# End of layer 1: a new order of tiles, T from scaled tiles, evictions in three operations, a last root without GpSimd

## The chip, the core and the metric

The kernel runs on one core of a Trainium2 chip. TensorE (PE) multiplies, VectorE (DVE), ScalarE (ACT) and GpSimd (POOL) do the elementwise work, SyncE (SP) mostly issues transfers. The metric is the device time of one execution in microseconds; the median of three is 2872.47 us.

## What is computed

A diffusion backbone of two layers over 1024 latent tokens of width 1024, with 256 context tokens. The change lies in the second layer, which has windowed attention and no context output; one helper of it, the output projection, is used by the first layer too. Of the reference, what follows the second layer's attention:

```python
def layer_norm(x, g, b):
    xf = x.astype(jnp.float32)
    mu = jnp.mean(xf, -1, keepdims=True)
    var = jnp.mean(jnp.square(xf - mu), -1, keepdims=True)
    return ((xf - mu) * lax.rsqrt(var + LN_EPS) * g + b).astype(x.dtype)

def modulate(x, shift, scale):
    return x * (1 + scale) + shift

def conv_ffn(h, w_up, conv_w, conv_b, w_down):
    u = h @ w_up
    L = u.shape[1]
    r = CONV_W // 2
    up = jnp.pad(u, ((0, 0), (r, r), (0, 0)))
    acc = conv_b
    for j in range(CONV_W):
        acc = acc + up[:, j:j + L] * conv_w[j]
    a, g = jnp.split(acc, 2, axis=-1)
    return (jax.nn.silu(g) * a) @ w_down
...
            y_lat, y_ctx = odd_mixer(h_lat, h_ctx, od_w_in[i], od_w_out[i], od_sink[i], cos, sin, ctx_out)
        x_lat = layer_norm(DN_ALPHA * x_lat + m_lat[2] * y_lat, ln_g[l, 0], ln_b[l, 0])
        f_lat = conv_ffn(modulate(x_lat, m_lat[3], m_lat[4]), ffn_w_up[l], ffn_conv_w[l], ffn_conv_b[l], ffn_w_down[l])
        x_lat = layer_norm(DN_ALPHA * x_lat + m_lat[5] * f_lat, ln_g[l, 1], ln_b[l, 1])
```

## The kernel before

Float32 values are multiplied as pairs: each operand is split into a high part (a cast to the matmul's type, on ACT) and a low part (value minus high part, a subtraction on DVE or POOL), and a product is three matmuls: high by high, high by low, low by high.

**Output projection** (`out_project`). The tokens are eight tiles of 128. For a tile t the mixer's output y is loaded in two halves into `yr` (L1425), cast to `yh` by ACT (L1426), and POOL subtracts into `yl` (L1427). 48 matmuls of 128x512 form two halves `o0` and `o1`. DVE evicts a half in three operations: times the gate (L1446), plus alpha times x (L1447), statistics (L1450). `ln` then forms the mean and the reciprocal root, which it calls rs (DVE L360, POOL L362 and L363), and normalises x (DVE L376; for the last tile half on ACT, L375). `finish` of the tile before, which calls `build_B1`, stands behind a tile's matmuls; for the last tile it stands in the middle of them. A scheduler orders this section's instructions on each engine from the program's order.

**Operand of the up product** (`build_B1`). The normalised tile is transposed by TensorE (L1728, tile `tr`) and modulated by ACT (L1734). Tiles 0 to 3 are the left and 4 to 7 the right half of the token axis; features are split too, so the operand has four blocks: `h3la` and `h3lb` (with `h` and `l` behind the name for the high and low part). For the seven products of a Strassen-like scheme, four differences T0 to T3 of the blocks are needed. They are formed when tile t of 4 to 7 is there, from its own modulated values and from the high and low parts of tile t - 4, six DVE operations (L1768 to L1773), and stored to DRAM; tile 7's stay on chip in `w` buffers. Later they are loaded again (`gk`, `go`, `ua`, `ug`), and split into T0h, T0l and so on (L1871, L1872).

After the last tile TensorE runs `first_x` (two products over tiles 0 to 3, which starts with L2928), the last tile's transposes, and `rest` (two further products).

**Up stage** (`ffn7`, from here on in an order written out by hand). 22 pairs of feature blocks; a pair is seven products of twelve matmuls (L1842) into tiles x, y, q, v. ACT and DVE form u from them (among others L2479, which q waits for), convolve (`centre` on ACT, `sides` on DVE, L2321), apply Silu (ACT, L2349), multiply (L2353), and `store` and `mix` form the sums that the down product reads, which `put` sends to DRAM through POOL's queue. Two pairs share a buffer, `gk` of the even and `go` of the odd one; slots 0 to 6 of the store are the seven products' left operands.

**Down stage.** 77 pieces (11 by seven products), each of twelve matmuls on four tiles (L2524). `load(j)` brings two pieces' right and left operands and splits them (right: L112 and L113, left: L2301 and L2302). The order of everything else is a table of jobs by the piece's number: `job(i, f)` issues f behind piece i. `evict` moves a result to z, in three operations (L2534, L2538, L2539), or with a saved part `vs` in four (L2536 to L2539). `end` is the final layer norm (L360, then POOL L362 and L363, then DVE L3088 and L3091, then the store L3093). The last nine pieces run tile by tile, 4 to 7, each followed by its eviction and `end`:

```python
            for t in range(4):
                for i in range(NS - last, NS):
                    mm(i, t)
                evict(4 + t, 0, Y[t])
                end(4 + t)
```

## Time and profile before

| | us |
|---|---|
| median of three runs | 2872.47 (2872.45 to 2876.41) |
| the profiled execution | 2874.48, its span 2872.6 |
| PE busy | 2747.7 (96% of the span) |
| DVE busy | 2145.0 (75%) |
| ACT busy | 1388.0 (48%) |
| POOL busy | 667.2 (23%) |

Times in rows count from the span's start. The section at hand runs from about 2110 to the end: projection to 2206, up stage to about 2640, down stage behind it. In the rows, `x12` is a count, and a bracket `[2.87 <-issue]` is how long the engine was idle before and what ended that. The ends of matmuls are modelled, so the spacing of starts (0.227 us for 128x512) is the surer measure.

### The profile page before, as it was taken

What the parts mean: (1) busy time and instruction counts of PE and PEld (TensorE: products, weight loads), DVE (VectorE), ACT (ScalarE), POOL (GpSimd) and SP (SyncE); (2) the same over time, 40 slices, a digit from 0 to 9 for tenths busy, and PEclk for the clock granted to TensorE, in tenths of its full rate; (3) what the DMA queues carried; (4) which work ended last, traced back from release to release, by engine and by line L of the source; (5) the groups of instructions that cost most, each with busy time, mean ns of one, the idle gap of its engine ahead of it and who ended that gap; (6) DMA issues with size and microseconds to landing.
All of it is one profiled execution on the core that took longest, in us unless ns stands there. A gap on an engine that the chain in (4) does not pass through costs nothing.

```text
span 2872.6 us, 45400 instructions
## 1 busy us (share of the span) xinstructions
PE 2747.7 (96%) x16724; PEld 2244.9 (78%) x16724; DVE 2145.0 (75%) x3852; ACT 1388.0 (48%) x2607; POOL 667.2 (23%) x948
## 2 busy tenths in 40 slices
PE   8999799899999999999999999999998999999997
PEld 6787577777789988888888888766677788888886
DVE  4765676667588777888878656677778888888778
ACT  4321255567435655455553344167743555445541
POOL 4501243354451000000001002255644011111002
PEclk9999899999999999999999999999999999999998
DMA  7568611032558753333458525652244355555962
GB/s 272 153 206 279 214 32 43 9 134 92 169 161 243 216 165 108 110 114 110 121 197 294 173 98 171 199 165 81 83 132 162 120 180 176 165 173 205 329 218 90
DMA packets 369222, 457.02 MB, mean 159 GB/s; under 512 B 26008, under 2 KB 265016, under 8 KB 367464
## 3 DMA queue, kind: packets, MB, share of 16 engines
q1 hardware_dynamic: 341512, 369.53, 40.5%
q0 software_dynamic: 24592, 82.89, 8.3%
q8 instruction: 131, 2.15, 0.3%
q10 hardware_dynamic: 2896, 1.70, 0.2%
q14 instruction: 91, 0.75, 0.1%
HBM read 338.11 MB, written 115.93 MB: 158 GB/s over the span
## 4 chain that ended last, share of the span: by engine, by line
PE 70%; DVE 9%; issue 9%; DMA 5%; ACT 4%; POOL 2%; SPq 0%; ACTq 0%; POOLq 0%; DVEq 0%
PE q L1842 8%; PE x L1842 7%; PE y L1842 7%; PE S L882 4%; PE v L1842 4%; PE pv L1027 3%; PE mm L405 3%; PE mm L407 3%; PE mm L406 3%; PE T L1013 3%; PE dy L2524 3%; PE d L407 3%; PE d L406 3%; PE d L405 3%; PE dx L2524 2%
## 5 line engine op out<-in xcount | busy, mean ns | idle before, releaser
L906 POOL TENSOR_SCALAR P<-P,rin 128x640 f32<-128x640 f32 (+3 forms) x288 | 253.0, 882 | 333.8 <-DVE rin L905 301.8
L1816 DVE TENSOR_TENSOR w<-raw,w 128x512 fp32r<-128x512 f32 x308 | 208.6, 691 | 90.1 <-ACT w L1814 89.9
L113 DVE TENSOR_TENSOR w<-raw,w 128x512 fp32r<-128x512 f32 x315 | 204.5, 689 | 86.4 <-ACT w L112 83.1
L112 ACT CAST w<-raw 128x512 fp32r<-128x512 f32 x315 | 183.4, 620 | 173.4 <-PE d L407 67.2
L882 PE MATMUL S<-k,q 64*128 64x256 f32 (+2 forms) x1824 | 194.9, 337 | 17.3 <-DVE nm L2862 8.3
L903 ACT ACTIVATE P<-P,nm 128x641 f32<-128x641 f32 (+4 forms) x208 | 161.5, 778 | 84.9 <-DVE nm L2862 43.9
L1814 ACT CAST w<-raw 128x512 fp32r<-128x512 f32 x308 | 182.3, 620 | 15.1 <-DVE raw L1821 9.9
L882 PEld LDWEIGHTS S<-k,q 64*128 64x128 f32 x1824 | 136.9, 187 | 54.5 <-issue 19.1
L893 ACT COPY PT<-T 128x512 f32<-128x512 f32 (+1 forms) x250 | 134.9, 566 | 82.7 <-PE T L1013 80.0
L1027 PE MATMUL pv<-PT,v 128*64 128x128 f32 x2016 | 132.9, 279 | 16.6 <-ACT PT L893 13.9
L1013 PE MATMUL T<-ident,P 128*128 128x128 f32 x1008 | 135.8, 282 | 9.5 <-POOL P L906 3.3
L1027 PEld LDWEIGHTS pv<-PT,v 128*64 128x64 f32 x2016 | 108.5, 137 | 42.7 <-ACT PT L893 23.2
L405 PE MATMUL d<-w,w 128*128 128x512 f32 x352 | 137.5, 391 | 0.0
L407 PE MATMUL d<-w,w 128*128 128x512 f32 x352 | 137.0, 389 | 0.0
L406 PE MATMUL d<-w,w 128*128 128x512 f32 x352 | 137.0, 389 | 0.0
L1013 PEld LDWEIGHTS T<-ident,P 128*128 128x128 f32 x1008 | 110.4, 142 | 29.8 <-issue 17.4
L891 DVE COPY PT<-T 128x512 f32<-128x512 f32 (+1 forms) x166 | 110.4, 666 | 31.0 <-PE T L1013 21.1
L905 DVE RECIPROCAL rin<-den 128x1 f32<-128x1 f32 x288 | 46.0, 161 | 112.1 <-ACT P L903 108.7
L1842 PE MATMUL q<-T3h,w 128*128 128x512 f32 x352 | 121.1, 405 | 7.6 <-DVE ug L2479 4.0
L2524 PE MATMUL dy<-w,w 128*128 128x512 f32 x528 | 120.7, 390 | 0.0
L1842 PE MATMUL q<-T2h,w 128*128 128x512 f32 x352 | 115.9, 390 | 2.3 <-ACT q L2461 1.8
L903 ACT ACTIVATE P<-P,mc 128x1280 f32<-128x1280 f32 (+1 forms) x80 | 94.7, 1186 | 46.0 <-DVE mc L1148 41.6
(450 smaller groups left out, 7779.6 us busy)
## 6 DMA issues: line engine op xcount, KB each, us to landing
raw<-in_up_dram SPq DMA_DIRECT2D x132, 512.0 KB
raw<-in_down_dram SPq DMA_DIRECT2D x59, 512.0 KB
raw<-g SPq DMA_DIRECT2D x44, 512.0 KB
raw<-G SPq DMA_DIRECT2D x38, 512.0 KB
araw<-in_ada_w_dram SPq DMA_DIRECT2D x32, 512.0 KB
raw<-in_w_in_dram SPq DMA_DIRECT2D x28, 512.0 KB
g<-cv POOLq DMA_DIRECT2D x22, 512.0 KB, 3.0
G<-go POOLq DMA_DIRECT2D x44, 256.0 KB, 2.7
```

Of the source, the lines that this page charges most:

```text
L113: (lo_eng or nc.vector).tensor_sub(lo, s, f32(hi))
L405: nc.tensor.matmul(ps, lh, rh, start=first, stop=False)
L406: nc.tensor.matmul(ps, lh, rl, start=False, stop=False)
L407: nc.tensor.matmul(ps, ll, rh, start=False, stop=last)
L882: self.nc.tensor.matmul(outs[a], q[r, x, qs], k[r, y, ks], start=(i == 0), stop=(i == 2))
L903: nc.scalar.activation(P[:, :m], P[:, :m], AF.Exp, bias=negm, scale=-1.0, accum_out=den)
L906: nc.gpsimd.tensor_scalar(P[:, :n], P[:, :n], rin, 1.0, ALU.mult, ALU.mult)
L1013: nc.tensor.transpose(ps[:, s * 128 : (s + 1) * 128], P[a][:, cols[i + x] : cols[i + x] + 128], self.ident,)
L1027: nc.tensor.matmul(O[a * HD : (a + 1) * HD], v_of(a, vts[i + x]), pT[:, s * 128 : (s + 1) * 128], start=(i + x == 0), stop=(i + x == m - 1 ...
L1816: nc.vector.tensor_sub(half(i, 1), src[i], f32(half(i, 0)))
L1842: nc.tensor.matmul(ps, w[:, a, s], r[b][:, k], start=first and k + i == 0, stop=k == 3 and i == 2, skip_group_check=True,)
L2524: nc.tensor.matmul(banks[q][t], ga[i][:, a, c], wd[i][:, b], start=q < 2 and f + k == 0, stop=f == HF - 1 and k == 2, skip_group_check=True,)
```

## The change

1. `out_project` drops `yr`: y is loaded into `yl` and the subtraction is done in place. The tiles of layer 1 run in the order 0, 4, 1, 5, 2, 6, 3, 7. The first layer's projection keeps its order and gets the load in place.
2. `build_B1`: the low part's subtraction (L1746) goes from POOL to DVE. The modulated values of a tile below 4 stay in a buffer `b` until tile t + 4 follows, and T is formed from these in four DVE operations. Only tile 7 keeps T on chip; tile 6 stores it as the others do.
3. `rest` begins with a Silu of one column, so the table of Silu is loaded there.
4. In an odd pair the sum for slot 0 and its store go from `store` to the start of `mix`, which in the instruction order is behind L2479.
5. Down stage: every seventh load's right operands lie in a pool of their own with two buffers, the left operands have seven buffers, loads run up to six ahead where they ran up to five, and reach the next depth sooner; the scaling of z (`scale`) and of the norm's rows (`alpha`) are early; `gated` multiplies the saved part by the gate and `shared` adds it to z before the evictions, which then take three operations each. The norm's rows of the last layer norm are loaded into the tiles of the first.
6. The table of Sqrt is loaded behind the last copies of ACT. The last tile has an `end` of its own: Sqrt on ACT, reciprocal on DVE, five operations on one column on ACT (one step that refines the root), and the last multiply and store in two halves on two queues. GpSimd takes no part in it.

The order of DVE at three places. First, tiles 6 and 7 in the projection: `hst<-o1` is the eviction of tile 7's right half; `hst` and `b` are modulated values. Before:

```order
L1768 TENSOR_TENSOR yh_23551<-hst_23534,h3lah_22713 128x512
L1769 TENSOR_TENSOR yh_23551<-yh_23551,h3lal_22714 128x512
L1745 CAST h3lbh_22715<-hst_23544 128x4x128
L1770 TENSOR_TENSOR yh_23551<-hst_23544,yh_23551 128x512
L1771 TENSOR_TENSOR yl_23552<-hst_23544,hst_23534 128x512
L1772 TENSOR_TENSOR yl_23552<-h3lbh_22715,yh_23551 128x512
L1773 TENSOR_TENSOR yl_23552<-yl_23552,h3lbl_22716 128x512
L1446 TENSOR_TENSOR hst_23586<-o_4548_23487,gate_22733 128x512
L1447 SCALAR_TENSOR_TENSOR x_23488<-x_23488,hst_23586 128x512
```

Now, with tile 3 ahead of tile 7:

```order
L1745 CAST h3lah_22695<-b_23502 128x4x128
L1746 TENSOR_TENSOR h3lal_22696<-b_23502,h3lah_22695 128x4x128
L1745 CAST h3lbh_22697<-b_23514 128x4x128
L1746 TENSOR_TENSOR h3lbl_22698<-b_23514,h3lbh_22697 128x4x128
L1446 TENSOR_TENSOR hst_23546<-o_4519_23457,gate_22715 128x512
L1447 SCALAR_TENSOR_TENSOR x_23458<-x_23458,hst_23546 128x512
```

Six T operations and a cast stood ahead of the eviction; two casts and two subtractions stand there now. Second, DVE from tile 7's T to T0l. Before:

```order
L1768 TENSOR_TENSOR w_23653<-hst_23636,h3lah_22713 128x512
L1769 TENSOR_TENSOR w_23653<-w_23653,h3lal_22714 128x512
L1745 CAST h3lbh_22715<-hst_23646 128x4x128
L1770 TENSOR_TENSOR w_23653<-hst_23646,w_23653 128x512
L1771 TENSOR_TENSOR w_23654<-hst_23646,hst_23636 128x512
L1772 TENSOR_TENSOR w_23654<-h3lbh_22715,w_23653 128x512
L1816 TENSOR_TENSOR w_23687<-raw_22956,w_23687 128x512
L1773 TENSOR_TENSOR w_23654<-w_23654,h3lbl_22716 128x512
L1816 TENSOR_TENSOR w_23690<-raw_22956,w_23690 128x512
L1872 TENSOR_TENSOR T0l_23717<-gk_23718,T0h_23716 128x2x4x128
```

Now (L1802 is L1816 of before, L1858 is L1872):

```order
L1761 TENSOR_TENSOR w_23613<-hst_23596,b_23502 128x512
L1745 CAST h3lbh_22697<-hst_23606 128x4x128
L1762 TENSOR_TENSOR w_23613<-hst_23606,w_23613 128x512
L1746 TENSOR_TENSOR h3lbl_22698<-hst_23606,h3lbh_22697 128x4x128
L1763 TENSOR_TENSOR w_23614<-hst_23606,hst_23596 128x512
L1764 TENSOR_TENSOR w_23614<-b_23514,w_23613 128x512
L1802 TENSOR_TENSOR w_23647<-raw_22934,w_23647 128x512
L1802 TENSOR_TENSOR w_23650<-raw_22934,w_23650 128x512
L1858 TENSOR_TENSOR T0l_23677<-gk_23678,T0h_23676 128x2x4x128
```

Ahead of T0l stand eight operations where nine stood, one of them the low part that POOL formed. Third, the last tile's eviction and norm on DVE. Before:

```order
L2534 TENSOR_TENSOR tt_28658<-dy_5059_27073,gate_27054 128x512
L2538 TENSOR_TENSOR z_5033_27041<-z_5033_27041,tt_28658 128x512
L2539 BN_STATS s_5041_27049<-z_5033_27041 128x6
L360 BN_AGGR mv_28662<-s_5041_27049 128x2
L3088 SCALAR_TENSOR_TENSOR z_5033_27041<-z_5033_27041,mv_28662,lg_27845 128x1024
L3091 SCALAR_TENSOR_TENSOR z_5033_27041<-z_5033_27041,rs_28664,lb_27846 128x1024
```

Now:

```order
L2527 TENSOR_TENSOR tt_28630<-dy_5028_27036,gate_27017 128x512
L2528 TENSOR_TENSOR z_5002_27004<-z_5002_27004,tt_28630 128x512
L2529 BN_STATS s_5010_27012<-z_5002_27004 128x6
L3088 BN_AGGR mv_28634<-s_5010_27012 128x2
L3091 TENSOR_SCALAR lv_28636<-mv_28634 128x1
L3092 RECIPROCAL ly_28637<-ly_28637 128x1
L3093 SCALAR_TENSOR_TENSOR z_5002_27004<-z_5002_27004,mv_28634,gb_5019_27027 128x1024
L3103 SCALAR_TENSOR_TENSOR z_5002_27004<-z_5002_27004,lr_28640,gb_5020_27028 128x512 x2
```

The reciprocal waits for ACT ahead of the wide operation, and the last multiply is two halves.

The diff, its context cut:

```diff
@@ -98,12 +98,12 @@
-    def split(self, src, n, shape=None, lo_eng=None):
+    def split(self, src, n, shape=None, lo_eng=None, pool=None):
...
         for s in src:
-            w = self.t(self.ring, [128, 2, 512], "w", R)
+            w = self.t(pool or self.ring, [128, 2, 512], "w", R)
             hi, lo = w[:, 0, :n], w[:, 1, :n]
@@ -1420,8 +1420,8 @@
                 for q in range(2):
-                    yr = self.t(st, [128, 4, 128], "yr", bufs=2)
                     s = slice(4 * q, 4 * q + 4)
+                    yr = f32(yl[:, s])
                     nc.sync.dma_start(yr, yv[:, s, t * 128 : (t + 1) * 128])
@@ -1728,7 +1728,7 @@
                 )
-            s = self.t(st, [128, 4, 128], "hst", bufs=3)
+            s = self.t(st, [128, 4, 128], "b" if t < 4 else "hst", bufs=2 if t < 4 else 3)
             for j in range(4):
@@ -1743,8 +1743,9 @@
             nc.vector.tensor_copy(h, s)
-            nc.gpsimd.tensor_sub(l, s, f32(h))
+            nc.vector.tensor_sub(l, s, f32(h))
         if t < 4:
+            self.b1 = sg
             return
@@ -1752,31 +1753,16 @@
             self.tlast = tt = [m[i // 2][:, i % 2] for i in range(4)]
-        elif t == NLAT - 2:
-            m = [
-                self.t(st, [128, KT, 128], x, bufs=2).rearrange("p (m k) j -> p m k j", m=2)
-                for x in ("yh", "yl")
-            ]
-            tt = [m[i // 2][:, i % 2] for i in range(4)]
         else:
...
             tt = [m[:, i] for i in range(4)]
-        b11, b21 = ([f32(v) for v in x] for x in (
-            (ah[:, :, o], al[:, :, o]), (bh[:, :, 0, o], bl[:, :, 0, o])
-        ))
+        b11, b21 = self.b1
         b12, b22 = sg
-        nc.vector.tensor_sub(tt[0], b12, b11[0])
-        nc.vector.tensor_sub(tt[0], tt[0], b11[1])
+        nc.vector.tensor_sub(tt[0], b12, b11)
         nc.vector.tensor_sub(tt[1], b22, tt[0])
         nc.vector.tensor_sub(tt[2], b22, b12)
-        nc.vector.tensor_sub(tt[3], b21[0], tt[1])
-        nc.vector.tensor_add(tt[3], tt[3], b21[1])
-        if t == NLAT - 2:
-            for i in range(2):
-                nc.gpsimd.dma_start(
-                    dT[2 * i : 2 * i + 2, :, t - 4].rearrange("m p k j -> p m k j"), m[i]
-                )
-        elif t < NLAT - 2:
+        nc.vector.tensor_sub(tt[3], b21, tt[1])
+        if t < NLAT - 1:
             nc.gpsimd.dma_start(dT[:, :, t - 4].rearrange("m p k j -> p m k j"), m)
@@ -2240,7 +2226,7 @@
     def ffn7(self, l, B, hps, T, dT, xsrc, gate_row, view, begin, finish, norm,
-             early=None, px=None):
+             early=None, px=None, warm=None):
@@ -2291,7 +2277,8 @@
                 nc.sync.dma_start(g[:, :m], Gv[:, s : s + m])
-                for i, w in enumerate(self.split([r[:, i] for i in range(m)], 512)):
+                pool = wp if j >= 3 and j % 7 == 6 else self.ring
+                for i, w in enumerate(self.split([r[:, i] for i in range(m)], 512, pool=pool)):
                     wd[s + i] = w
@@ -2357,13 +2344,13 @@
                     put(6, f, x[:, 512:])
-                    k = half["k"]
-                    nc.vector.tensor_add(k[:, 512:], k[:, 512:], x[:, 512:])
-                    put(0, f, k[:, 512:])
...
                     f, x, k = s.i // 2, s.a, half["k"]
-                    if s.i % 2 == 0:
+                    if s.i % 2:
+                        nc.vector.tensor_add(k[:, 512:], k[:, 512:], x[:, 512:])
+                        put(0, f, k[:, 512:])
+                    else:
                         nc.vector.tensor_sub(k[:, :512], k[:, :512], k[:, 512:])
@@ -2501,7 +2488,8 @@
             zp = es.enter_context(self.pool("fz"))
-            gp[0] = es.enter_context(self.pool("fgs", bufs=6))
+            gp[0] = es.enter_context(self.pool("fgs", bufs=7))
+            wp = es.enter_context(self.pool("fws", bufs=2))
             pd = es.enter_context(self.pool("fd", space=PSUM))
@@ -2527,14 +2515,16 @@
-            def evict(t, n, ps, v=None):
+            def gated(t):
+                nc.vector.tensor_mul(vs[t], vs[t], gate[:, 512:])
+
+            def shared(t):
+                nc.vector.tensor_add(z[t][:, 512:], z[t][:, 512:], vs[t % 4])
+
+            def evict(t, n, ps):
                 s = slice(n * 512, (n + 1) * 512)
                 tt = self.t(tt2, [128, 512], "tt")
-                if v is None:
-                    nc.vector.tensor_mul(tt, ps, gate[:, s])
-                else:
-                    nc.vector.tensor_add(tt, v, ps)
-                    nc.vector.tensor_mul(tt, tt, gate[:, s])
+                nc.vector.tensor_mul(tt, ps, gate[:, s])
                 nc.vector.tensor_add(z[t][:, s], z[t][:, s], tt)
@@ -2566,22 +2556,25 @@
                 job(8 + 3 * t, lambda t: nc.sync.dma_start(z[t], xsrc(t)), t)
-                job((20 + 3 * t) if t < 4 else (46 + 2 * (t - 4)), scale, t)
-            job(16, alpha)
-            job(36, begin, es, pd)
+                job(14 + 3 * t, scale, t)
+                job(37 + 2 * t, shared, t)
+            job(12, alpha)
+            job(36, begin, es, pd, gb)
             job(HF - 1, copies, vs, Y)
...
                 job(3 * HF + 1 + 2 * t, evict, t, 0, X[t])
-                job(5 * HF + 2 * t, evict, t, 1, Y[t], vs[t])
+                job(33 + t, gated, t)
+                job(5 * HF + 2 * t, evict, t, 1, Y[t])
                 job(5 * HF + 1 + 2 * t, end, t)
-                job(6 * HF + t // 2, evict, 4 + t, 1, X[t], vs[t])
+                job(6 * HF + t // 2, evict, 4 + t, 1, X[t])
+            job(6 * HF + 1, warm)
             ahead = 2
...
                 if i % 2 == 0:
-                    n = i // 2 + min(5, 2 + i // 12)
+                    n = i // 2 + min(6, 2 + i // 10)
                     while ahead <= n:
@@ -2930,12 +2923,14 @@
             def rest():
+                warm = self.t(st, [128, 1], "warm")
+                nc.scalar.activation(warm, self.mhalf[:, :1], AF.Silu)
                 for p in range(2):
...
             self.out_project(
-                io["w_out1"], d["yT1"], list(range(8)),
+                io["w_out1"], d["yT1"], [0, 4, 1, 5, 2, 6, 3, 7],
                 rows("x2"), lambda t: gate, finish, st, wx, pp,
@@ -3073,15 +3068,47 @@
-        def begin_o(es, pd):
+        def begin_o(es, pd, gb):
             st = box["st"] = es.enter_context(self.pool("fino"))
-            box["g"] = self.t(st, [128, D], "lg")
-            box["b"] = self.t(st, [128, D], "lb")
+            box["g"], box["b"] = gb
             self.bcast(box["g"], io["ln_g"][1, 1])
             self.bcast(box["b"], io["ln_b"][1, 1])
+            box["c"] = self.t(st, [128, 4], "lc")
+            for i, v in enumerate((LN_EPS, -1.25, 1.875, 1.0)):
+                nc.vector.memset(box["c"][:, i : i + 1], v)
+
+        def warm_o():
+            nc.scalar.activation(
+                self.t(box["st"], [128, 1], "warm"), box["c"][:, 3:], AF.Sqrt
+            )
+
+        def last_o(t, z, s6):
+            st, c = box["st"], box["c"]
+            mv = self.t(st, [128, 2], "mv", bufs=3)
+            nc.vector.bn_aggr(mv, s6.rearrange("p a b -> p (a b)"))
+            ve, y, e, p, rs = (self.t(st, [128, 1], "l" + x) for x in ("v", "y", "e", "p", "r"))
+            nc.scalar.activation(y, mv[:, 1:2], AF.Sqrt, bias=c[:, :1])
+            nc.vector.tensor_scalar(ve, mv[:, 1:2], LN_EPS, 1.0, ALU.add, ALU.mult)
+            nc.vector.reciprocal(y, y)
+            nc.vector.scalar_tensor_tensor(
+                z, z, mv[:, 0:1], box["g"], ALU.subtract, ALU.mult
+            )
+            nc.scalar.activation(e, y, AF.Identity, scale=y)
+            nc.scalar.activation(e, e, AF.Identity, scale=ve)
+            nc.scalar.activation(p, e, AF.Identity, bias=c[:, 1:2], scale=0.375)
+            nc.scalar.activation(p, p, AF.Identity, bias=c[:, 2:3], scale=e)
+            nc.scalar.activation(rs, p, AF.Identity, scale=y)
+            for h, q in enumerate((nc.sync, nc.scalar)):
+                s = slice(h * 512, (h + 1) * 512)
+                nc.vector.scalar_tensor_tensor(
+                    z[:, s], z[:, s], rs, box["b"][:, s], ALU.mult, ALU.add
+                )
+                q.dma_start(io["out"][t * 128 : (t + 1) * 128, s], z[:, s])
...
             st = box["st"]
+            if t == NLAT - 1:
+                return (lambda: last_o(t, z, s6)), None
             mv, rs = self.stats(st, s6)
@@ -3095,7 +3122,7 @@
         self.ffn7(1, h2l, [hl, pxc], {}, d["T1"], rows("x3"), a[1, 0, 5], view1, begin_o, finish_o,
-                  (io["ln_g"][1, 0], io["ln_b"][1, 0]), early=self.early, px=px)
+                  (io["ln_g"][1, 0], io["ln_b"][1, 0]), early=self.early, px=px, warm=warm_o)
         self.finish_dbg()
...
     def finish_dbg(self):
```

## Prediction

> **What bounds the kernel now.** I read the windows by stage first, then the waits of TensorE in the stretch that the change touches, then the time rows around each wait, and last the chain at the end. The windows give busy time per engine; the columns are PE, PEld, DVE, ACT, POOL, granted clock, DMA share, GB/s.
>
> ```profile
> 2110.00:2260.00 150.00, 134.81 (x598) 108.89 (x597) 115.56 (x154) 60.19 (x126) 53.56 (x56) 0.97 0.44 146
> 2260.00:2640.00 380.00, 379.75 (x1665) 311.24 (x1663) 332.38 (x436) 195.36 (x298) 60.30 (x112) 1.00 0.54 171
> 2640.00:2793.00 153.00, 152.18 (x669) 125.37 (x669) 115.73 (x139) 79.05 (x114) 3.77 (x7) 1.00 0.80 283
> 2793.00:2854.00 61.00, 60.93 (x269) 50.13 (x267) 55.13 (x74) 14.33 (x21) 13.30 (x16) 1.00 0.29 104
> ```
>
> From 2260 to 2854 TensorE is never idle (379.75 of 380, 152.18 of 153, 60.93 of 61). So a microsecond that leaves the front (2110 to 2260, where 15.2 us of PE are missing and the clock is 0.97) reaches the end unless a feeder runs out, and behind 2854 nothing is left but the last tiles' tail. What TensorE waits for in the front:
>
> ```profile
> PE v L1842 <- DVE T0l L1872: 4.6, 1, 4.6
> PE q L1842 <- DVE ug L2479: 3.0, 1, 3.0
> PE tr L1728 <- issue: 2.9, 1, 2.9
> ...
> PE tr L1728 <- DVE x L376: 0.7, 1, 0.7
> ```
>
> These four are 11.2 of the 15.2 us, and DVE stands behind each.
>
> **Part A, the transposes (L1728).** The waits of 0.7 and 2.9 stand ahead of the transposes of a normalised tile: the first of tile 6, in the middle of tile 7's matmuls, the second of tile 7. Below are DVE's and TensorE's rows around the second.
>
> ```profile
> 2199.97 0.67 DVE L1768 TENSOR_TENSOR yh<-hst,h3lah 128x512 f32<-128x512 f32 x1
> ...
> 2205.26 0.68 DVE L1446 TENSOR_TENSOR hst<-o,gate 128x512 f32<-128x512 f32 x1
> ```
>
> ```profile
> 2200.45 0.39 PE L2928 MATMUL y<-h3lah 128*128 128x512 f32 x1
> ...
> 2209.38 1.06 PE L1728 MATMUL tr<-ident,x 128*128 128x128 f32 x8 [2.87 <-issue]
> ```
>
> TensorE left tile 7 at 2200.45 (L2928 is the first matmul of what follows, the product on tiles 0 to 3), but the eviction of tile 7's right half (L1446) stood on DVE behind tile 6's whole T, from 2199.97 to 2205.26. In the new order tile 3 is ahead of tile 7, has no T, and hands DVE two casts and two subtractions; the eviction then starts near 2201, 4 us sooner, against a wait of 2.9. Both waits go: 3.6 us. Bounds: 0 if the four short operations of tile 3 come as late as tile 6's did, 3.6 at most. That product on tiles 0 to 3 now reads tile 3, made just before; if its low part were late, that would wait in place of this, but DVE reaches it ahead of the eviction. I take 3.6.
>
> **Part B, T0l (L1872).** T0l is the low half of the first of the four T, read by tile 0 to 3's v product; a quarter of it comes from tile 7. DVE's rows, and TensorE's wait:
>
> ```profile
> 2211.64 0.69 DVE L1768 TENSOR_TENSOR w<-hst,h3lah 128x512 f32<-128x512 f32 x1 [2.37 <-ACT hst L1734]
> ...
> 2213.99 1.80 DVE L1771 TENSOR_TENSOR w<-hst,hst 128x512 f32<-128x512 f32 x1
> ```
>
> ```profile
> 2221.19 0.50 PE L1842 MATMUL v<-T0l,w 128*128 128x512 f32 x1 [4.55 <-DVE T0l L1872]
> ```
>
> From tile 7's first T operation to TensorE's start DVE runs without a gap, 2211.64 to 2221.19. Two subtractions like L1768 go (0.69 each, 1.3 together by start to start). L1771 takes 1.80 while GpSimd subtracts the low part; with that subtraction on DVE it should take the 0.68 of its neighbours, 1.1 less, and the subtraction itself adds 0.7. Net 1.7, which I take; bounds 0.6 (if L1771 stays at 1.80) and the whole 4.55.
>
> **Part C, the Silu table and the clock.** ACT's rows in the second pair of the up stage:
>
> ```profile
> 2248.03 1.28 ACT L2349 ACT_TABLE_LOAD   x1 [2.41 <-DVE cv L2321]
> 2249.32 1.06 ACT L2349 ACTIVATE cv<-cv 128x1024 f32<-128x1024 f32 x1
> ```
>
> The load stands between DVE's convolution and Silu, and DVE's product, the q ahead of TensorE (L2479) and the wait of 3.0 stand behind it. Issued early it falls into a stretch of ACT that waits for y anyway, so 1.28 goes and the wait becomes 1.7. [...] I stay with 1.28.
>
> The second cost of the wait is the clock. Two windows with a granted clock of 0.50, then pieces of the chain:
>
> ```profile
> 2221.79:2225.20 3.41, 3.41 (x10) 2.65 (x9) 3.41 (x5) 0.00 (x0) 0.00 (x0) 0.50 0.90 312
> 2252.50:2259.30 6.80, 5.90 (x14) 4.64 (x15) 3.85 (x7) 0.38 (x1) 1.12 (x2) 0.50 0.20 77
> ```
>
> ```profile
> 2253.40 5.49 PE q L1842 x12
> 2258.88 3.01 PE x L1842 x12
> ...
> 2275.49 2.95 PE q L1842 x12
> ```
>
> Behind the waits of 4.55 and 3.0 TensorE ran at 0.50 for 3.41 and 6.80 us; behind 2.87 it did not. The 5.90 us of work in the second stretch cost 2.95 too much (5.49 + 3.01 against 5.44 gives 3.06). A wait of 1.7 is below the 2.87 that left the clock alone, so I take 2.9 here; bounds 0 and 3.06. B's wait stays near 2.9, where either may happen: I count nothing, with 1.7 (half of 3.41) as the upper bound. [...]
>
> **Part D, odd pairs of the up stage.** DVE's rows in one odd pair, and the last of the slow q pieces of the chain beside a normal one:
>
> ```profile
> 2312.40 0.69 DVE L2361 TENSOR_TENSOR gk<-gk,go 128x512 f32<-128x512 f32 x1
> 2313.01 0.68 DVE L2479 TENSOR_TENSOR ug<-ua,q 128x512 f32<-128x512 f32 x1
> ```
>
> ```profile
> 2579.78 2.72 PE y L1842 x12
> 2582.50 2.98 PE q L1842 x12
> ```
>
> The sum for slot 0 (L2361) stands ahead of the operation on which q waits, and in eight odd pairs, from 2275.49 (2.95) to 2582.50 (2.98), q's twelve matmuls show some 0.22 above 2.72. The sum moves behind L2479, 0.6 by start to start, which covers 0.22: 8 x 0.22 = 1.8. It adds work before the next pair's convolution writes the same buffer, whose store must have landed first:
>
> ```profile
> G<-go POOLq DMA_DIRECT2D x44, 256.0 KB, 2.7
> ```
>
> In the new order some six DVE operations of 0.6 lie between the two, about 3.6 us by estimate, so 2.7 fits, narrowly; a landing at 4.6 would cost each even pair 1, which ACT's idle share there (195 busy of 380) would partly take. I take 1.6; bounds -1 and 1.8.
>
> **Part E, the tail.** TensorE's last group, two split pieces of the chain, and DVE's rows of evictions and of the last root:
>
> ```profile
> 2828.84 25.09 PE L2524 MATMUL dy<-w,w 128*128 128x512 f32 x110
> ```
>
> ```profile
> 2828.74 1.28 DVE w L113 x2
> 2830.02 1.14 DVE w L2302
> ```
>
> ```profile
> 2843.35 0.68 DVE L2534 TENSOR_TENSOR tt<-dy,gate 128x512 f32<-128x512 f32 x1
> ...
> 2860.23 0.68 DVE L2534 TENSOR_TENSOR tt<-dy,gate 128x512 f32<-128x512 f32 x1
> ...
> 2864.64 1.28 DVE L3091 SCALAR_TENSOR_TENSOR z<-z,rs,lb 128x1024 f32<-128x1024 f32 x1 [0.72 <-POOL rs L363]
> ```
>
> TensorE ends at 2853.9, and the last eviction starts only at 2860.2: 6.3 us of DVE backlog. Tile 4's (2843.35) is late by 8.2, its matmuls being done near 2835.1 (25.09 us for 110 matmuls is 0.228 each, and a tile's last nine pieces are 27 of them, 6.2 us; three tiles behind tile 4 make 18.5 to 18.8 before 2853.9). The change takes one of four operations out of eight right-half evictions (8 x 0.70 = 5.6) and, with loads one deeper, moves one load's splits (1.28 + 1.14 = 2.4) ahead of 2793. That is 8.0 of the 8.2. What is moved ahead, twelve operations of 0.7 and the splits, 11 us, lies in the window 2640:2793, where DVE is busy 115.73 of 153 and its cover is 37 us. From tile 4 on DVE needs 5.6 a tile ((2860.23 - 2843.35)/3) and TensorE 6.2, so the rest of the backlog melts, and the last eviction starts when TensorE ends: 6.2 us (bounds 0 and 6.3).
>
> Behind it the end changes too:
>
> ```profile
> L3204 POOLq DRAIN  x3: 46/93/7784, 2864.0 to 2872.3; - x3
> ```
>
> ```profile
> 2865.95 0.33 SPq L3093 DMA_DIRECT2D out_dram<-z  x1
> ```
>
> ```profile
> L2758 ACT ACTIVATE warm<-snk 128x1 f32<-128x1 f32 x1 | 0.2, 203 | 0.5 <-DVE snk L2618 0.5
> ```
>
> GpSimd's closing drain starts behind its last root (2864.0) and takes 7.78, to 2871.8, which closes the span at 2872.6; the last store, issued at 2865.95, has 5.9 us until then. Now GpSimd's last root is tile 6's, 6 us sooner, and the last store should close the span. The new root is a chain of six small ACT operations and a reciprocal. ACT's 128x1 takes 0.20 in the row; with the semaphore between them I estimate 1.4 (seven of 0.2) to 2.8 (twice that) for the chain, against 2.1 on GpSimd now (2864.64 - 2860.23, less three operations of 0.7 and an aggregate of 0.2), and most of it lies beside a DVE operation of 1.28. Two halves of 0.69 replace one of 1.28. So the last DVE operation comes 5.8 after the eviction's start instead of 5.7. If the store then takes about 3 us (the row of 256 KB has 2.7) and the close 1.3, the end stands 10.1 behind the eviction's start and no longer 12.4: 2.3, and halves land sooner, so I take 2.5; bounds 0 (something else closes as late) and 3.
>
> Layer 0's projection goes through the same in-place load; its tiles have two buffers as before, and I count 0.
>
> **Sum.** 3.6 + 1.7 + 1.3 + 2.9 + 1.6 + 6.2 + 2.5 = 19.8 us. The profiled execution took 2874.48 for a span of 2872.6, so its span would become 2852.8; it lies 2.0 above the median of 2872.47, which the same sum takes to 2852.7. I say 2853.
>
> **Rivals.**
> (a) The front gives little: the clock still halves behind the shorter wait, the last T loads rather than DVE decide T0l, and the odd pairs hand their wait on to even ones. That is 2.9 + 1.7 + 1.6 back: 2859. [...]
> (b) The backlog stays: the moved operations or the deeper loads wait for buffers, and DVE enters 2793 as late as now. 6.2 back: 2859. For it: DMA share 0.80 in 2640:2793; against it: 37 us of DVE cover. With (a): 2865.
> (c) Slower: y now lands in the low-part buffer, which TensorE must have released.
>
> ```profile
> 2107.80 7.48 DMA yr<-yT
> 2115.30 0.63 ACT yh L1426
> ```
>
> ```profile
> 2128.00:2200.00 72.00, 71.32 (x344) 59.45 (x343) 56.90 (x72) 25.54 (x66) 39.09 (x40) 1.00 0.36 126
> ```
>
> ```profile
> L1427 POOL TENSOR_TENSOR yl<-yr,yh x32: 1282/1296/1802, 753.4 to 2177.0; 128x512 fp32r<-128x512 f32 x32
> ```
>
> A tile of 56 matmuls takes 11.7 us (72 x 56/344). The slowest landing seen, 7.48, with a cast of 0.63 and two subtractions of 1.3 makes 10.7: it fits by 1.0. Were landings over 11.8, six tiles would each wait 3.3 and eat the sum; at 14 the kernel would be 6 x 5.5 - 19.8 = 13 slower, 2886. Against it: DMA share 0.36 here.
> (d) The new root is no faster and some queue still closes late: E's second part 0, and 2855, within the forecast's own range.
>
> **How the numbers follow.** Forecast 0.57 (own range 2849 to 2856), (a) 0.15, (b) 0.15, both 0.05, (c) 0.04, more than forecast (the whole wait of B and its slow clock, 4.6) 0.04. From 2848 to 2865 lie over 8 in 10. What a measurement can tell from no change is about 0.2%, 5.7 us: faster needs under 2866.7. All but (c) and a worse sum of (a) and (b) are faster: 0.91, same 0.05, slower 0.04.
>
> **What would show it.** Right: no wait ahead of tr; v behind T0l waits about 3; no ACT table load between cv and Silu, q waits 1.7 at clock 1.00; odd q at 2.72; the last eviction within 1 us of TensorE's end; the span's end some 10 us behind TensorE's. Wrong: a new wait of o on yl, of gk's convolution on a store, or DVE late by several us at the last eviction.

## The result and the profile after

| | before | changed |
|---|---|---|
| median, first set of runs | 2873.09 (2872.45 to 2876.41) | 2860.31 (2854.05 to 2863.08) |
| median, second set | 2875.33 (2868.07 to 2881.16) | 2859.45 (2857.22 to 2865.95) |
| span of the profiled execution | 2872.6 | 2852.3 |

The ratio is 0.9947 (95% interval 0.9933 to 0.9962), the second time 0.9951 (0.9935 to 0.9966). So the change is worth 12.8 and 15.9 us by medians, where 19.8 had been forecast. The profiled execution of the changed kernel ended at 2852.3, half a microsecond from the forecast span of 2852.8, but it is the shortest of the eleven. The median lies 7.3 above the forecast of 2853: outside the forecast's own 2849 to 2856, inside the wider 2848 to 2865. It is nearer to the 2859 of rivals (a) and (b), though the rows below show what neither of them says. What the 7 us are is the question of the experiments.

The table cuts the traces at five points of TensorE's order that all these kernels share, so that a piece can be compared whatever the pieces ahead did. Times are differences of the starts of matmuls (the last row: to the end of the span). "First projection matmul" is, in both layers, the first one of the second tile; the first tile's y is brought in by other code, and its matmuls stand ahead. The third column is a second trace of the changed kernel.

| stretch, us | before | changed | changed, second trace |
|---|---|---|---|
| start to the first layer's first projection matmul | 753.3 | 748.8 | 755.5 |
| to the last up matmul of the context behind it | 290.3 | 296.2 | 297.9 |
| to the first projection matmul of layer 1 | 1072.4 | 1072.2 | 1072.6 |
| to the last down matmul | 737.6 | 725.2 | 726.0 |
| to the end of the span | 19.05 | 9.92 | 9.92 |

In the part that the prediction worked on (the last two rows) 21 us are gone in both traces, against 19.8. In the second row, at the first layer's projection, 5.9 and 7.6 us have come. The first row is, but for the first load of y, code that no edit touches, and differs by 6.7 between two executions of one kernel; in the 14 traces of this study it lies between 748.8 and 755.5. The profiled execution was lucky there: its first row is 4.6 shorter than before's, which hides most of the 5.9 lost in the second. That its span came out where it was forecast is chance.

The windows of the changed kernel, with the columns of the prediction's table (PE, PEld, DVE, ACT, POOL, clock, DMA share, GB/s):

```profile
2110.00:2260.00 150.00, 141.02 (x635) 114.94 (x634) 117.62 (x168) 66.31 (x135) 33.80 (x43) 0.98 0.49 157
2260.00:2635.00 375.00, 374.84 (x1653) 309.71 (x1652) 329.50 (x434) 191.98 (x294) 61.53 (x114) 1.00 0.54 174
2635.00:2790.00 155.00, 155.00 (x685) 128.36 (x684) 128.25 (x162) 82.32 (x118) 3.90 (x6) 1.00 0.82 288
```

PE is busy 141.02 of the front's 150 (134.81 before). In the third row DVE has taken on the work that was moved ahead: 128.25 of 155, with TensorE never idle. TensorE's waits in the front:

```profile
PE v L1828 <- DVE T0l L1858: 3.5, 1, 3.5
PE q L1828 <- DVE ug L2466: 2.0, 2, 1.7
PE o L405 <- ACT yh L1426: 1.5, 1, 1.5
PE q L1828 <- ACT q L2448: 1.3, 2, 0.7
PE o L407 <- POOL yl L1427: 0.7, 1, 0.7
```

Both waits of `tr` are gone, T0l stands at 3.5 (4.6 before), and q's wait in the second pair at 1.7 (3.0). The tail, from the chain of waits:

```profile
2812.83 29.93 PE dy L2512 x132
2842.76 0.02 issue
2842.79 0.70 DVE tt L2527
...
2847.46 0.75 DVE z L3103
2848.22 0.66 DVEq L3231
```

TensorE's last group ends 2842.76 and the last eviction starts 2842.79: no backlog is left (6.3 before). The last column operation of the root ends 4.7 behind that, and the chain no longer passes GpSimd: its closing drain takes 7.78 as before, but starts at 2840.47 and is over 4 us ahead of the end. Between stand the root's small operations, of which the first and the last two on ACT:

```profile
2845.21 0.29 ACT L3090 ACTIVATE ly<-mv,lc 128x1 f32<-128x1 f32 x1 [30.26 <-DVE mv L3088]
...
2846.72 0.39 ACT L3099 ACTIVATE lp<-lp,lc,le 128x1 f32<-128x1 f32 x1
2847.14 0.29 ACT L3100 ACTIVATE lr<-lp,ly 128x1 f32<-128x1 f32 x1
```

### The profile page after: what moved, and what is told of

It reads as the page before. It is cut to its first block, busy times and chain, and to the rows that moved or that the text cites. A ratio compares the mean times of both kernels' runs of the same rounds, so it can differ in the third digit from the quotient of the medians.

```text
span 2852.3 us, 45396 instructions
## 1 busy us (share of the span) xinstructions
PE 2743.7 (96%) x16724; PEld 2244.4 (79%) x16724; DVE 2147.1 (75%) x3867; ACT 1392.9 (49%) x2616; POOL 642.6 (23%) x933
## 4 chain that ended last, share of the span: by engine, by line
PE 73%; issue 9%; DVE 8%; DMA 5%; ACT 4%; POOL 2%; SPq 0%; ACTq 0%; DVEq 0%; POOLq 0%
PE q L1828 8%; PE x L1828 8%; PE y L1828 8%; PE dy L2512 4%; PE S L882 4%; PE v L1828 4%; PE mm L405 3%; PE pv L1027 3%; PE mm L407 3%; PE mm L406 3%; PE T L1013 3%; PE dx L2512 3%; PE d L406 3%; PE d L405 3%; PE d L407 3%
## 5 line engine op out<-in xcount | busy, mean ns | idle before, releaser
L1802 DVE TENSOR_TENSOR w<-raw,w 128x512 fp32r<-128x512 f32 x308 | 209.7, 695 | 82.5 <-ACT w L1800 82.2
```

The lines of the kernel that those rows point to most:

```text
L1802: nc.vector.tensor_sub(half(i, 1), src[i], f32(half(i, 0)))
```

## The experiments

Each kernel is the changed one with the edit shown, if nothing else is said. "The long stretch" is from the first projection matmul of layer 1 (as in the table) to the last down matmul. In the diffs, `...` stands for lines left out.

**The changed kernel again.**

> The changed kernel a second time. Its profiled execution ended at 2852.3, but its five times run from 2854 to 2863. Theory (the sum of the prediction): the stretch from the projection's first matmul to the end of the span is 735 us again (756.6 before), give or take 2 for one half-clock stretch behind T0l, and times differ by half-clock stretches ahead of 2110, which the change does not touch; a median between 2853 and 2861. Rival: the changed part itself is unsteady, and this stretch comes out 4 to 9 us longer than 735 in some executions.

The long stretch is 726.0 and the end 9.92, together 736.0 (735.1 in the first trace). It is steady; its start was 9 us later than in the first trace (2125.97 against 2117.14), of which 6.7 are in code ahead of everything changed and 1.7 in the first layer's projection. The stretch and the median came as the theory has it, with one thing it did not say: the first layer's stretch was long in both. That the rest is half clock ahead of 2110 does not show: the granted clock of the first row is 0.98 in both traces, and TensorE is idle there for 62.1 us in the first and 65.4 in the second.

**The front alone**: the edits to the projection, T, the Silu table and the odd pair's sum; down stage and last roots as before.

> The projection, T, the early Silu table and the odd pair's sum as changed; the down stage and the last roots as before. Theory: the parts A to D are worth 11 us by themselves, so from the projection's first matmul to the last down matmul 726 us (737.6 before, 725.2 with the whole change), and from there to the end 19 as before; span near 2861.5. Rival: the front only runs ahead and the down stage gives it back at its feeders: 735 or more to the last down matmul.

The long stretch is 727.6 and the end 19.05: the front's gain is 10 by itself and nothing of it is given back. But the median fell only to 2869.7 against 2875.3 (ratio 0.9987, 0.9976 to 0.9998), where 11 were expected: 5.4 are missing, and they are not in this stretch.

**The tail alone**: the edits to the down stage and the last roots only.

> Only the down stage and the last roots as changed; the front as before. Theory: nothing of A to D, 737 us from the projection's first matmul to the last down matmul, and 9.9 from there to the end where it was 19.05; span near 2863.5. Rival: the backlog was melted by what the front gave DVE; then the last eviction starts 2 us or more behind the last matmul and 12 or more remain to the end.

The long stretch is 738.4, the end 9.82; median 2865.5 against 2875.3, 9.8 less (0.9963, 0.9949 to 0.9977). All that was expected is there. The chain of this kernel:

```profile
2834.79 19.28 PE dy L2526 x85
2854.09 0.70 DVE tt L2541
```

The last eviction follows TensorE at once although the front is the old one, so the tail's gain does not hang on the front.

**Old order of tiles**, old projection with staging, T in six operations, the low part on GpSimd; Silu early, the odd pair's sum as changed.

```diff
...
-                io["w_out1"], d["yT1"], [0, 4, 1, 5, 2, 6, 3, 7],
+                io["w_out1"], d["yT1"], list(range(8)),
```

> The changed kernel with the old projection, the old order of tiles and T in six operations; the Silu table is still loaded early. Theory: A and B come back: the waits of 0.7 and 2.9 ahead of the transposes and 4.6 ahead of T0l stand again, 3.6 + 1.1 = 4.7 us more than the changed kernel in the stretch from the projection's first matmul to the end (740). Rival: a shorter wait only moves half-clock stretches about, and the stretch is within 2 us of 735.

```profile
PE v L1842 <- DVE T0l L1872: 4.5, 1, 4.5
PE tr L1728 <- issue: 2.9, 1, 2.9
PE q L1842 <- DVE ug L2480: 1.7, 1, 1.7
PE q L1842 <- ACT q L2462: 1.7, 2, 1.0
PE o L405 <- ACT yh L1426: 1.2, 1, 1.2
PE tr L1728 <- DVE x L376: 0.7, 1, 0.7
```

The waits of 4.5, 2.9 and 0.7 are back as forecast, and the long stretch with the end is 743.1, some 7.5 more than with the order (735.1 and 736.0), where 4.7 were expected. To tile 7's transposes it is 93.1 against 89.4 and 89.7, the 3.6 of part A. From there to q on T3 it is 25.9 (25.6 and 23.7 with the order), and from q on T3 to the first down matmul 403.8, 1.4 to 3.1 more, which was not followed. Yet its median was 2862.0, within 3 us of the changed kernel's 2859.5. A kernel that lacks 7.5 us of gain and is hardly slower must win somewhere else, and this one differs in one more thing: it stages y, in both layers.

**The first layer.** With that, the second row of the table above was read in all traces. It is 290.3, 291.7 and 290.7 in the three kernels with staging (before, tail alone, old order) and 296.2, 297.9 and 296.1 in the three that load y in place. The group of DVE's L1447 between 740 and 870 (x is the count, then busy time, mean ns of one), before and changed:

```profile
L1447 DVE SCALAR_TENSOR_TENSOR x<-x,hst 128x512 f32<-128x512 f32 x20 | 21.4, 1073 | 0.5
```

```profile
L1447 DVE SCALAR_TENSOR_TENSOR x<-x,hst 128x512 f32<-128x512 f32 x20 | 30.6, 1536 | 0.5
```

The rows of the changed kernel at the first half of the last tile but one show what a long one stands beside:

```profile
843.39 0.68 DVE L1446 TENSOR_TENSOR hst<-o,gate 128x512 f32<-128x512 f32 x1
843.77 0.81 POOL L1715 DMA_DIRECT2D T<-tt  x1 [0.93 <-DVE tt L1714]
844.10 3.57 DVE L1447 SCALAR_TENSOR_TENSOR x<-x,hst 128x512 f32<-128x512 f32 x1
844.60 2.52 POOL L1427 TENSOR_TENSOR yl<-yl,yh 128x512 fp32r<-128x512 f32 x2
```

Before, around the same eviction:

```profile
836.93 2.98 POOL L1427 TENSOR_TENSOR yl<-yr,yh 128x512 fp32r<-128x512 f32 x2 [2.42 <-ACT yh L1426]
...
845.82 0.69 DVE L1447 SCALAR_TENSOR_TENSOR x<-x,hst 128x512 f32<-128x512 f32 x1
```

GpSimd's two subtractions for the last tile run back to back, 2.52 us, and DVE's eviction beside them, recorded as started 0.5 ahead of them, takes 3.57, where the median of the 20 is 0.69. How the one holds up the other, the rows do not show. Before, the same subtractions started at 836.93, right behind ACT's cast and well ahead of this eviction, and met only one of the tile before (837.24, 1.52 us). Loaded in place, y is fetched only when TensorE has left the tile that had the buffer (load issued at 831.46, cast done at 837.63). The cast is there in time, but GpSimd comes to the subtractions only at 844.60: in the instruction order they now stand behind the T of an earlier tile (its store, 843.77), which they stood ahead of. So it is the place on GpSimd that has moved, beside DVE's evictions. That the scheduler puts them there because the load is late is my reading; no run changes that place alone.

Two kernels test this. **Staging in the first layer only:**

```diff
-                    yr = f32(yl[:, s])
+                    yr = f32(yl[:, s]) if mid else self.t(st, [128, 4, 128], "yr", bufs=2)
```

> The changed kernel, but the first layer's projection again loads y into the staging tile yr; layer 1 loads in place. The traces of the kernels with the load in place show 296 to 298 us from the first layer's first projection matmul to the last up matmul of the context behind it, where the kernels with staging show 290 to 292, and there DVE's L1447 takes 1.58 on average where it took 1.07. Theory: the late load puts GpSimd's two subtractions of a tile back to back beside DVE's evictions, which wait for them; with staging that stretch returns to 291, L1447 to about 1.1, and the median falls by 5 against the changed kernel. Rival: the difference is half-clock stretches that fall there by chance; then the stretch stays at 295 or more, or L1447 stays at 1.5.

The stretch is 292.3, L1447 is back:

```profile
L1447 DVE SCALAR_TENSOR_TENSOR x<-x,hst 128x512 f32<-128x512 f32 x20 | 21.7, 1089 | 0.6
```

The median is 2855.2 against 2873.1 before (ratio 0.9932, 0.9918 to 0.9945): 17.9 less, where the changed kernel had 12.8 and 15.9. The long stretch is 726.2 and the end 9.82 as in the changed kernel. **The load in place as the only edit to the kernel before:**

> The kernel before with one edit: y loaded into yl and subtracted in place, in both layers. Theory: 5 to 6 us more than before in the first layer (296 from the first projection matmul to the last up matmul of the context), L1447 at 1.5 or more there, some 0 to 2 more in layer 1; median 5 to 7 above before. Rival: the load in place costs nothing by itself and the first layer's loss comes from another part; then 290 to 292 and a median equal to before.

```profile
L1447 DVE SCALAR_TENSOR_TENSOR x<-x,hst 128x512 f32<-128x512 f32 x20 | 29.4, 1472 | 0.5
```

The stretch is 297.3, and the median 2883.2 against 2873.1 (1.0036, 1.0023 to 1.0050): 10 slower, where 5 to 7 were expected. In layer 1 it also lost: 95.6 from the first projection matmul to tile 7's transposes against 93.4 before, of which 3.4 us of half clock that fell there account for up to 1.7. So the load in place costs 5.5 in the first layer by nine traces with it (296.1 to 297.9, mean 296.8) and five without (290.3 to 292.3, mean 291.3), which do not overlap. Part of it shows at the product behind the projection, whose weights load behind the last tile's norm. TensorE's wait there, before and changed:

```profile
PE d L405 <- ACT w L112: 3.6, 2, 2.1
```

```profile
PE d L405 <- ACT w L112: 6.1, 2, 4.7
```

That is 2.5 of the 5.5; 1.4 more are new short waits on yl and x. Over all, TensorE is idle for 7.3 to 7.8 us of this stretch in the nine and for 2.8 to 3.8 in the five, 4.2 more in the mean. Half clock does not explain the difference: with staging in the first layer 6.8 us of it fell into the stretch, as in four of the nine, and it is 292.3 against 296.7 to 297.3 there.

**Without the early Silu table.**

```diff
             def rest():
-                warm = self.t(st, [128, 1], "warm")
-                nc.scalar.activation(warm, self.mhalf[:, :1], AF.Silu)
```

> The changed kernel without the early Silu: the table is loaded ahead of the first Silu of the up stage again. Theory: q then waits 3.0 (1.7 with the early load) in the second pair, and TensorE runs half clock for 3.4 to 6.8 us behind it: 3 to 4.3 us more between q on T3 and the first down matmul (400.7 to 402.6 with the change), so 404 to 406. [...]

```profile
2253.96 0.50 PE L1828 MATMUL q<-T3h,w 128*128 128x512 f32 x1 [2.98 <-DVE ug L2466]
```

```profile
2254.50:2257.90 3.40, 3.40 (x9) 2.62 (x8) 2.42 (x5) 0.00 (x0) 0.54 (x1) 0.51 0.20 77
```

The wait is 2.98 again and TensorE runs at half clock behind it, for 3.4 us here and 6.8 before. From q on T3 to the first down matmul it takes 404.3, against 400.7 to 403.8 (mean 402.0) in the nine traces with the table early and the odd pair's sum moved. That is 2.3 more than the mean, from one trace; by the rows it should be 3.0, 1.3 for the table and 1.7, half of the 3.4. Behind the wait of 1.7 TensorE kept the full clock in all ten traces with the early table; behind the wait of 3.0 it lost it in three of four without (not in the one with the load in place alone).

**Last root on GpSimd.**

```diff
-            if t == NLAT - 1:
-                return (lambda: last_o(t, z, s6)), None
...
-            job(6 * HF + 1, warm)
```

> The changed kernel, the last tile's root on GpSimd again and one store of the whole tile, as for the others. Theory: GpSimd's closing drain, 7.8 behind its last operation, ends the span again: the last eviction starts at TensorE's end as in the changed kernel, the drain begins some 3.8 behind that, and 12.4 remain from the last down matmul to the end where the changed kernel has 9.9. Rival: what GpSimd cost was the backlog alone; then 10 remain.

```profile
L3228 POOLq DRAIN  x3: 46/93/7784, 2851.9 to 2860.2; - x3
```

12.8 us remain from the last down matmul (2847.7) to the end, 2.9 more than in the changed kernel. GpSimd's drain starts with its last root at 2851.9 and takes 7.78 once more. The theory holds.

**Two weight splits behind T0l**, with staging in the first layer:

```diff
                         make_T(0)
+                        if pre:
+                            self.some_parts(early[0][1], [4])
                         make_T(1)
+                        if pre:
+                            self.some_parts(early[0][1], [3, 5, 6])
```

(and the same call is taken out of `rest`).

> The changed kernel with staging in the first layer, and two weight splits of DVE moved from ahead of T0l to behind it. Theory: v's wait for T0l falls from 3.5 to 2.3; up to 0.6 of it comes back ahead of y on T1; the stretch from the projection's first matmul to the end is 734 to 736, and the median 16 to 21 below before, at least as low as with the staging alone (19). Rival: the next thing in line (T0h on ACT, or the loads of T) is as late as DVE was, v still waits 3.5, and nothing changes.

```profile
2214.10 0.50 PE L1828 MATMUL v<-T0l,w 128*128 128x512 f32 x1 [1.69 <-DVE T0l L1858]
2217.34 0.50 PE L1828 MATMUL y<-T1h,w 128*128 128x512 f32 x1 [0.46 <-ACT T1h L1857]
2218.77 0.50 PE L1828 MATMUL y<-T1l,w 128*128 128x512 f32 x1 [0.93 <-DVE T1l L1858]
2226.20 0.80 PE L1828 MATMUL q<-T2h,w 128*128 128x512 f32 x1 [4.67 <-ACT q L2452]
```

T0l's wait fell by 1.8, more than forecast, and 1.4 came back ahead of T1 and 4.0 ahead of q, where ACT was now late with a copy behind casts. The long stretch is 730.0, 4 longer. Both theories missed: the thing behind was not as late as DVE, it was later. The median, 2856.2 against 2872.8 (0.9941, 0.9927 to 0.9954), does not beat the staging alone.

**Four operations an eviction again**, loads one deeper.

```diff
...
-                job(37 + 2 * t, shared, t)
...
-                job(33 + t, gated, t)
-                job(5 * HF + 2 * t, evict, t, 1, Y[t])
+                job(5 * HF + 2 * t, evict, t, 1, Y[t], vs[t])
...
-                job(6 * HF + t // 2, evict, 4 + t, 1, X[t])
+                job(6 * HF + t // 2, evict, 4 + t, 1, X[t], vs[t])
```

> The changed kernel, but the saved part joins each right-half eviction again (four operations each), with nothing scaled or added ahead; loads stay one deeper. Theory: eight operations of 0.7 return to the stretch in which DVE is behind, of which it makes up 0.5 a tile: the last eviction starts 3 to 4.5 us behind the last matmul (0.4 in the changed kernel), and 13 to 14 remain to the end, where it has 9.9. Rival: the deeper loads alone give enough slack, 10 to 11 remain.

```profile
2852.75 0.68 DVE L2528 TENSOR_TENSOR tt<-dy,gate 128x512 f32<-128x512 f32 x1
```

The last down matmul started at 2848.4; the eviction starts 3.9 behind TensorE's end, where it was 6.3 before, and 13.8 remain. So the deeper loads, with the scalings that stay early, take 2.4 off the lag when they act alone.

**Loads five ahead again**, three operations.

```diff
-                    n = i // 2 + min(6, 2 + i // 10)
+                    n = i // 2 + min(5, 2 + i // 12)
```

> The changed kernel with loads at most five ahead, as before; evictions in three operations. Theory: one load's splits, 2.4 us of DVE, come back into the tail, of which 1.5 is made up over the last tiles: 10.5 to 11 from the last down matmul to the end instead of 9.9. Rival: DVE has slack enough and it is 9.9.

```profile
2846.49 0.69 DVE L2527 TENSOR_TENSOR tt<-dy,gate 128x512 f32<-128x512 f32 x1 [0.41 <-PE dy L2512]
```

9.82 to the end, and the last eviction waits for TensorE. The rival holds: once the operations are out of the evictions, the deeper loads add nothing at the tail. Its long stretch is 728.3, 2.3 to 3.1 longer than the changed kernel's; 10.2 us of half clock fell into it, and whether the loads have a part in this is open.

**The odd pair's sum in its old place.**

```diff
                 def store(s):
...
+                    k = half["k"]
+                    nc.vector.tensor_add(k[:, 512:], k[:, 512:], x[:, 512:])
+                    put(0, f, k[:, 512:])
                 def mix(s):
...
-                    if s.i % 2:
-                        nc.vector.tensor_add(k[:, 512:], k[:, 512:], x[:, 512:])
-                        put(0, f, k[:, 512:])
...
```

> The changed kernel with the sum for slot 0 in its old place, ahead of the operation that q waits for. Theory: each odd pair's q shows 0.22 above 2.72 again, 1.8 us in all between q on T3 and the first down matmul (400.7 to 402.6 with the change), so 402.5 to 404.4. Rival: the excess of 0.22 lies in the modelled rows and not in time; then 401 to 402.5 with the excess there or gone.

```profile
2576.72 2.97 PE q L1828 x12
```

405.2 from q on T3 to the first down matmul, above the ranges of theory and rival, and 3.1 more than the mean of the nine traces above. q's excess (2.97 for 2.72) is back in each odd pair; in two pairs q waited 0.9 besides, in the second of which the changed kernel's second trace waits too. Between the second pair and the last but one, the products' starts lie 2.6 to 3.7 us in all beyond 2.72 each in the four kernels without the edit (before, tail alone, load in place alone, this one), and 0.3 to 1.6 in the ten with it. By the means of the two groups the edit is worth some 2.5, more than was forecast.

## Why the prediction was right, and where it was not

**Part A** (3.6 forecast): both waits are gone and stay gone in all traces with the new order; the old order brings 2.9 and 0.7 back. From the first projection matmul to tile 7's transposes 93.4 became 89.4 and 89.7, 3.7 to 4.0 less. Right in mechanism and size.

**Part B** (1.7 forecast, wait down to 2.9): the wait fell by 1.1, to 3.48. DVE's rows show where the rest went:

```profile
2208.75 0.69 DVE L1761 TENSOR_TENSOR w<-hst,b 128x512 f32<-128x512 f32 x1 [3.91 <-ACT hst L1734]
2210.15 0.43 DVE L1745 CAST h3lbh<-hst 128x512 fp32r<-128x512 f32 x1 [0.70 <-ACT hst L1734]
...
2211.69 0.69 DVE L1763 TENSOR_TENSOR w<-hst,hst 128x512 f32<-128x512 f32 x1
...
2216.44 0.68 DVE L1858 TENSOR_TENSOR T0l<-w,T0h 128x512 fp32r<-128x512 f32 x1
```

L1763 takes 0.69 where L1771 took 1.80, as forecast. But the cast of the right half now waits 0.70 for ACT, with one operation ahead of it where two stood: the chain that I took to be DVE's alone had ACT close behind. And the clock decides what it is worth. Behind this wait the profiled execution ran at half clock for 6.8 us:

```profile
2216.20:2223.00 6.80, 5.82 (x14) 4.56 (x15) 5.07 (x8) 2.65 (x6) 0.00 (x0) 0.50 0.86 258
```

In the second trace of the same kernel the wait is 3.5 too, up to 2226.29, and the clock stays at 1.00:

```profile
2224.00:2232.00 8.00, 5.18 (x21) 3.98 (x22) 7.55 (x12) 4.91 (x9) 0.00 (x0) 1.00 0.70 217
```

From tile 7's transposes to q on T3 it takes 25.6 in the one and 23.7 in the other, 26.0 before; in the nine traces with the wait of 3.5 it takes 25.2 in the mean, so B is worth 0.8, and 0.2 to 2.3 by whether half clock follows. No run shows what decides it when the wait is the same.

**Parts C and D** (1.3 + 2.9 + 1.6 forecast, 5.8): from q on T3 to the first down matmul 408.4 became 400.7 and 402.4, 6.1 to 7.7. Undone singly, C costs 2.3 and D 3.1 by one trace each, and D some 2.5 by all traces. C's table and the 1.7 of wait came as forecast; its half clock was 3.4 us in the experiment rather than the 6.8 of the trace before, and none in the kernel with the load in place alone, so C is worth 1.3 to 4.2 by what follows the wait. The reason given for it, that 1.7 is shorter than the 2.87 that left the clock alone, was thin: behind the same 2.9 half clock came in one of four traces. Behind 1.7 it came in none of ten, and why is not shown. D was sized by the excess of q alone, in eight pairs where the rows of the chain show nine, and came out above its bound of 1.8. B fell short and D went over: that the sum of A to D fits is in part luck.

**Part E** (6.2 + 2.5 forecast): 19.05 became 9.92, 9.1. The eviction's lag fell by the forecast 6.2. The operations taken out of the evictions are enough for it: without the deeper loads no lag is left. The deeper loads without them leave 3.9, which is the prediction's own sum: 8.2 late at tile 4, less their 2.4, less the 1.9 made up from there to the last tile (8.2 to 6.3 before). The same sum leaves 0.7 with the operations alone, where no lag was measured, so the two gains do not add up: the loads' 2.4 is a reserve here and not a gain beside the other. With both undone, as in the front alone, 19.05 remain. The root's part was 2.9 for 2.5. The 1.3 us of its sum for the close were an estimate without a row; the changed kernel's last two stores are issued at 2848.24 and 2848.91, and the span ends 3.4 behind the second, where store and close had been put at 4.3 together.

**The step that failed** is the one line "Layer 0's projection goes through the same in-place load; its tiles have two buffers as before, and I count 0." It cost 5.5. Of the prediction's signs of being wrong the first one showed, faintly and in that layer: o waited on yl three times, 1.7 us in all, where it had waited once for 1.0. I had asked whether TensorE would wait for y, found that a tile's time covers the load, and stopped; rival (c) asked the same of layer 1. What the load moved was GpSimd's subtraction, into the time of DVE's evictions, and part B of the same prediction had used just this collision (L1771, 1.80 beside GpSimd) as a gain. With 21.1 won and 5.5 lost, 15.6 are left, and the medians show 12.8 and 15.9; with staging in the first layer, 17.9.

## What to carry to other kernels

A load that goes straight into its working buffer starts only when that buffer is released, and what stands behind it on the slower engines moves with it; here GpSimd's subtractions came to stand beside DVE's evictions, one of which took 3.57 for 0.69. Look at who works at the new place, and look at every caller of the helper, not only at the one in the section being tuned. When executions of one kernel differ by as much as the effect looked for, cut the traces at points that both kernels share and compare pieces: the first 750 us here differ by 6.7 from execution to execution. Take a new prefetch depth or a moved operation back singly before believing its share, and remember that two edits against one backlog need not add up: here one of them was enough.

## What was not expected of the hardware

The length of a wait of TensorE does not say by itself whether half clock follows. Over the 14 traces, at the waits named above: behind 1.7 us in none of eleven, behind the 2.9 ahead of the transposes in one of four, behind 3.0 in three of four, behind 3.5 in eight of nine, behind 3.7 to 4.7 in five of five, for 3.4 us or 6.8. The changed kernel shows both behind a wait of 3.48: a clock of 0.50 for 6.8 us in its first trace, of 1.00 in its second. The forecast had put the step between 2.87 and 3.0, from one trace. These are counts of the waits that the traces hold; no run sets where a wait falls, and what decides between 2.9 and 3.5 is open.

A DVE operation of 0.69 us took up to 3.6 beside two GpSimd subtractions of 2.5 together. A 128x1 operation of ACT in the new root takes 0.29 to 0.39, and the chain of six with the reciprocal 2.2 (2845.21 to 2847.43), the same as GpSimd's two operations (2.1); what the new root saves is GpSimd's drain of 7.8 at the end of the program.
